# Mixture-of-experts stage of a decoder trunk: earlier conversion of the next down piece, combining between gate pieces, and a fifth pair of part buffers in place of a ring slot

## The chip, the cores and the metric

One core of one Trainium2 chip. The metric is the device time of one execution in microseconds; lower is better. The kernel before was timed in three runs.

## The reference, cut to what matters

Two layers of a decoder trunk on 256 tokens of width 1024, all in float32. Each layer has a mixer (attention beside a gated delta rule) and a channel mixer; the channel mixer of the second layer, which is what the change touches, sends each token to 2 of 8 experts:

```python
def swiglu(x, w_gate, w_up, w_down):
    return (jax.nn.silu(x @ w_gate) * (x @ w_up)) @ w_down

def moe_ffn(x, router_w, w_gate, w_up, w_down):
    logits = jnp.einsum('td,de->te', xf, router_w).astype(jnp.float32)
    top_val, top_idx = lax.top_k(logits, TOP_K)
    gates = jax.nn.softmax(top_val, axis=-1)
    ...
    y = y * w_buf[:, None].astype(y.dtype)
    out = jax.ops.segment_sum(y, tok_buf, num_segments=T)
```

An expert has two matrices of 1024 x 3584 (gate, up) and one of 3584 x 1024 (down).

## The kernel before

**Two parts of a weight.** TensorE multiplies in a rounded float32 form. To keep the full precision each weight is converted into two parts: ScalarE copies the raw weight to the rounded form, `wh` (L173), and VectorE subtracts it from the raw weight, which gives the rest, `wl` (L176). The activations are split the same way. A product with a weight is then TensorE's `wh` times both parts of the activation and `wl` times the first part. `halves` (L163) does this for one raw piece in two halves, each into a pair of buffers `wh`, `wl` from `wpool`, which has four pairs (`WB`).

**Loads.** `load` (L148) brings one raw piece into a slot: seven slots of `ring`, and in the expert stage also five of `ring2`, taken in the order of the string `SLOTS` (`r` and `x`). A slot is free again when VectorE has made the last `wl` of what lay in it. All loads are issued by SP in program order.

**The expert stage.** `experts` runs eight jobs, one an expert, in the order 0, 1, 4, 2, 5, 3, 6, 7 of the experts ranked by load. A wide job gives its tokens 128 rows; the three *narrow* ones (ranks 1 to 3) have at most 64 tokens and put the two parts of the activations side by side into one 128-wide operand, so that a weight half takes four matmuls of 448 columns instead of six. Each job has two chunks (`c`) of 1792 of the 3584 hidden columns. A chunk is: gate, eight rows `k` of 128 x 1792 (`in_pieces`), in banks `mm` and `gd` of PSUM; Silu copies of the four banks into `hh` (L1183); up, eight rows likewise; the product of both on VectorE (L1205); `to_features`, TensorE transposes of `hh` with their split into `hT` (L1131 to L1134).

**The pending down product.** The down product of a chunk is not made at once. It is kept in `pend` and its seven pieces of 2 x 1024 columns (`down_pieces`) are put between the gate and the up of the next chunk and behind them: `more()` takes the next piece, three of them around the Silu copies, the others after up.

**Copies of second parts.** In a narrow job the second parts' results lie in the upper 64 rows of the banks. The last row of gate and of up (`k = 7`) is not converted: TensorE multiplies the raw weights in full float32 into the lower 64 rows (`raw` in the trace). Just ahead of that, `leads` (L1108) lets ScalarE copy the upper rows out of the four banks (`room`, L1115, pinned in program order); four matmuls with a shifted identity (`move`) add them to the lower rows later. The bank's raw product waits for its room copy, because both touch that bank.

**Combining.** When the last down piece of an expert is done (in the first chunk of the next job), `combine` (L1086) splits the two result banks into `ys` (L1088, L1089), multiplies them with the transposed mask `DT` back to token order, and adds them, scaled, to `x_in` (L1095). Then `transposed` makes the next `DT`. The steps of `to_features` are kept as a list, `side`, and one is taken after each row of the next gate.

**Order.** The program is scheduled at build time: each engine gets one queue in a fixed order, which follows the order of the code as far as the scheduler's own estimate finds an instruction ready. Instructions wrapped in `pin` keep program order among themselves.

Of the kernel before, what the change touches and what calls it, by code (L numbers as in the profile page):

```python
# [10 lines left out]
F32R = mybir.dt.float32r  # L11
# [6 lines left out]
P = 128  # L18
# [17 lines left out]
C_COLS = C_SMALL * P + 32 + 6 * 32  # L36

RING = 7
RING2 = 5
SLOTS = "rrrrrxxxrrxx"  # L40
CHUNK = 1792
BANK = CHUNK // 4
NARROW = 3
# [24 lines left out]
def trunk(ctx, tc, x, positions, w_in, conv_w, a_log, dt_bias, gdn_norm_w, lam_q1, lam_k1, lam_q2, lam_k2,  # L68
# [7 lines left out]
    wpool = ctx.enter_context(tc.tile_pool(name="wpool", bufs=WB))  # L76
# [5 lines left out]
    def nm(s):  # L82
        cnt[0] += 1
        return f"{s}_{cnt[0]}"


    def bank(tag):
        return ps.tile([P, 512], F32, tag=tag, name=nm("ps_" + tag))
# [52 lines left out]

    WC, WH = 2048, 1040
    extra = []
    turn = [0]
    fence_high = [None]
    fence = [None]

# [15 lines left out]
    def halves(ld, cut=1, count=2):  # L163

        raw, nk, cols = ld
        m = nk * cols // count
        for i in range(count):
            wh = wpool.tile([P, WH], F32R, tag="wh", name=nm("wh"))
            wl = wpool.tile([P, WH], F32R, tag="wl", name=nm("wl"))
            n = m // (cut if i else 1)  # L170
            for c in range(0, m, n):
                w = raw[:, i * m + c:i * m + c + n]
                high = S.activation(wh[:, c:c + n], w, AF.Copy)  # L173
                if fence_high[0] is not None:
                    order(high, fence_high[0])
                low = V.tensor_tensor(wl[:, c:c + n], w, wh[:, c:c + n].bitcast(F32), op=ALU.subtract)  # L176
                if fence[0] is not None:
                    order(low, fence[0])
            yield i * (nk // count), wh, wl
# [796 lines left out]
    def experts(xs, jobs, mp, ring2, rest, first):  # L976
# [52 lines left out]
        def transposed(n):  # L1029
            Dt = mp.tile([P, NB, P], F32R, tag="ys", name=nm("D"))  # L1030
            slots(Dt, jobs[n], True)
            DT = mp.tile([P, NB, P], F32R, tag=f"DT{n % 2}", name=nm("DT"), bufs=1)
            pt = bank("a")
            for b in range(NB):
                PE.transpose(pt[:, b * P:(b + 1) * P], Dt[:, b].bitcast(F32), ident)
            V.tensor_copy(DT.rearrange("p b t -> p (b t)"), pt[:, 0:NB * P])
            return DT

# [24 lines left out]
        def down_pieces(n, c, first=0, parts=1, cut=1):  # L1063

            wd = weights(n, 2)[c * CHUNK:(c + 1) * CHUNK].rearrange("(p j) d -> p j d", j=NF)
            for f in range(first, NF, 2):
                yield [(f + j, wh, wl) for j, wh, wl in piece(wd[:, f:f + 2, :], 2, D, parts, cut if f == NF - 2 else 1)]

        def down(subs, n, c, hT, py):
            for f, wh, wl in subs:  # L1070
                K, k = NC * NF, c * NF + f
                if jobs[n][3]:
                    x_ = hT[:, f].rearrange("p c s -> p (c s)")
                    for w in (wh, wl):
                        for i, o in enumerate(py):
                            mm(o, x_, w[:, i * 512:(i + 1) * 512], k == 0 and w is wh, k == K - 1 and w is wl)
                else:
                    for w in (wh, wl):
                        for c_ in range(2 if w is wh else 1):
                            for i, o in enumerate(py):  # L1080
                                mm(o, hT[:, f, c_], w[:, i * 512:(i + 1) * 512], k == 0 and w is wh and c_ == 0,
                                   k == K - 1 and w is wl)

        def combine(n, py, DT):
            for i in range(2):
                ys = mp.tile([P, 2, 512], F32R, tag="ys", name=nm("ys"))  # L1086
                yh, yl = ys[:, 0], ys[:, 1]
                S.activation(yh, py[i], AF.Copy)  # L1088
                V.tensor_tensor(yl, py[i], yh.bitcast(F32), op=ALU.subtract)  # L1089
                for b in range(NB):  # L1090
                    pt = bank("a")
                    mm(pt, DT[:, b], yh, True, False)
                    mm(pt, DT[:, b], yl, False, True)
                    o = x_tok[:, b, i * 512:(i + 1) * 512]
                    V.scalar_tensor_tensor(o, pt, jobs[n][2][:, b], o, op0=ALU.mult, op1=ALU.add)  # L1095

        regs = {}

# [9 lines left out]
        def leads(banks):  # L1108

            hi = slice(64, P)  # L1110
            moves = []

            room = mp.tile([P, 4, BANK], F32R, tag=f"xg{(xg_turn[0] + 1) % 2}", name=nm("room"), bufs=1)
            for i, p in enumerate(banks):
                pin(S.activation(room[hi, i], p[hi, :], AF.Copy))  # L1115
                moves.append(lambda o=room[hi, i], p=p: mm(p[0:64, :], shift[hi, 0:64], o, False, True))
            return moves
# [24 lines left out]
        pend = None  # L1142
        side = []
# [5 lines left out]
        for n, job in enumerate(jobs):  # L1149
            narrow = job[3]  # L1150
            rows = slice(0, 64) if narrow else slice(0, P)
            xg = xgs.pop(n)
            x32 = as_one(xg) if narrow else None
            wg, wu = (weights(n, i).rearrange("(k p) c -> p k c", p=P) for i in range(2))
            for c in range(NC):
                banks = gu_banks()
                for k, f in enumerate(first or ()):
                    products(banks, xg, narrow, k, f)
                moves = ()
                for sub in in_pieces(wg, c, len(first or ()), narrow):  # L1160
                    if narrow and sub[0] == KD - 1:
                        moves = leads(banks)
                    products(banks, xg, narrow, *sub, x32)
                    if side:
                        side.pop(0)()
                first = None
                fence[0] = fence_high[0] = None
                while side:
                    side.pop(0)()
                hh = mp.tile([P, CHUNK], F32, tag="hh", name=nm("hh"))  # L1170
                downs = down_pieces(pend[0], pend[1]) if pend else iter(())

                def more():
                    subs = next(downs, None)
                    if subs:
                        down(subs, *pend)

                more()
                for move in moves:
                    move()  # L1180
                more()
                for i, p in enumerate(banks):
                    pin(S.activation(hh[rows, i * BANK:(i + 1) * BANK], p[rows, :], AF.Silu))  # L1183
                more()
                banks = gu_banks()
                if c == NC - 1 and groups and n + 1 not in xgs:
                    group = groups.pop(0)
                    tiles, side = dispatch([jobs[g] for g in group])
                    xgs.update(zip(group, tiles))
                moves = ()  # L1190
                for sub in in_pieces(wu, c, 0, narrow):
                    if narrow and sub[0] == KD - 1:
                        moves = leads(banks)
                    products(banks, xg, narrow, *sub, x32)
                    if side:
                        side.pop(0)()
                while side:
                    side.pop(0)()
                more()
                for move in moves:  # L1200
                    move()
                more()
                for i, p in enumerate(banks):
                    h = hh[rows, i * BANK:(i + 1) * BANK]
                    pin(V.tensor_tensor(h, h, p[rows, :], op=ALU.mult))  # L1205
                for subs in downs:
                    down(subs, *pend)
                if pend and pend[1] == NC - 1:
                    combine(pend[0], pend[3], DT)
                if c == 0:  # L1210
                    DT = transposed(n)
                    py = [bank("b"), bank("b")]
                hT, side = to_features(hh, narrow)
                pend = (n, c, hT, py)
        _, where, gate, _ = job
        while side:
# [5 lines left out]
        subs = [(f0 + f, wh, wl) for subs in down_pieces(n, c, NF - TAIL, 2, 2) for f, wh, wl in subs]  # L1222
# [187 lines left out]
                xT = finish(fp, *dense_ffn(0, xT, fp), ln2_g, ln2_b, l)  # L1410
    pre_ctx.close()
    with tc.tile_pool(name="ring2", bufs=RING2, reuse_waits="tile") as ring2, \
            tc.tile_pool(name="mp", bufs=1, side="right", reuse_waits="tile") as mp:
        extra.append(ring2)
        turn[0] = len(first)
        moe(xs, pl, first, mp, ring2)

# [26 lines left out]
```

## Time and profile before

| what | us |
|---|---|
| median of three runs | 1523.3 |
| the three runs | 1520.12, 1523.3, 1524.71 |
| profiled execution, its own time | 1522.21 |
| span of its profile, first to last instruction | 1520.1 |

The span is shorter than the time of the same execution by what lies around it. The expert stage takes about the last two thirds of the span. In the profile an engine is busy while it works on an instruction; a gap ahead of an instruction is named with what ended it. PE is TensorE's matmuls, PEld its weight loads, DVE VectorE, ACT ScalarE, SP the engine that issues the loads. Who ended a wait is inferred from semaphores and can be wrong where the engine or load that is named had long been done.

### The profile page before, as it was taken

What the parts mean: (1) busy time and instruction counts of PE and PEld (TensorE: products, weight loads), DVE (VectorE), ACT (ScalarE), POOL (GpSimd) and SP (SyncE); (2) the same over time, 40 slices, a digit from 0 to 9 for tenths busy, and PEclk for the clock granted to TensorE, in tenths of its full rate; (3) what the DMA queues carried; (4) which work ended last, traced back from release to release, by engine and by line L of the source; (5) the groups of instructions that cost most, each with busy time, mean ns of one, the idle gap of its engine ahead of it and who ended that gap; (6) DMA issues with size and microseconds to landing.
All of it is one profiled execution on the core that took longest, in us unless ns stands there. A gap on an engine that the chain in (4) does not pass through costs nothing.

```text
span 1520.1 us, 24270 instructions
## 1 busy us (share of the span) xinstructions
PE 1466.2 (96%) x8864; PEld 1227.9 (81%) x8864; DVE 1228.5 (81%) x1609; ACT 1068.5 (70%) x1553; POOL 23.8 (2%) x37
## 2 busy tenths in 40 slices
PE   8999999999999999999999999999999999999995
PEld 8968899998978889866688876588876678888884
DVE  5887655556796789988899888899888889898985
ACT  5747444456657388877787786887887778778773
POOL 1100000000100000000000000000000000000000
PEclk9999999999999899999999999999999999999998
DMA  9534455546532589998999999999999999999860
GB/s 327 204 113 124 157 192 194 185 123 215 170 103 105 194 325 366 337 399 316 396 415 339 365 360 344 395 391 351 380 350 370 352 381 405 340 348 369 310 281 32
DMA packets 89127, 433.95 MB, mean 285 GB/s; under 512 B 7816, under 2 KB 9992, under 8 KB 74912
## 3 DMA queue, kind: packets, MB, share of 16 engines
q1 hardware_dynamic: 87808, 428.54, 76.0%
q0 software_dynamic: 1184, 3.71, 0.8%
q8 instruction: 73, 1.20, 0.3%
q14 instruction: 62, 0.51, 0.1%
HBM read 431.17 MB, written 1.05 MB: 284 GB/s over the span
## 4 chain that ended last, share of the span: by engine, by line
PE 79%; DVE 9%; ACT 5%; DMA 4%; issue 2%; SPq 0%; DVEq 0%; ACTq 0%
PE ps_mm L101 23%; PE ps_gd L101 23%; PE ps_b L101 22%; PE ps_a L101 9%; DVE wl L176 6%; ACT wh L173 2%; DMA raw<-in_moe_w_up_dram 2%; DMA raw<-in_moe_w_down_dram 2%; PE ps_a L1131 2%; ACT hh L1183 1%; DVE hh L1205 0%; ACT room L1115 0%; DVE x_in L1095 0%; PE ps_mm L562 0%; DVE hT L1134 0%
## 5 line engine op out<-in xcount | busy, mean ns | idle before, releaser
L176 DVE TENSOR_TENSOR wl<-raw,wh 128x896 fp32r<-128x896 f32 (+2 forms) x851 | 938.8, 1144 | 199.3 <-ACT wh L173 182.6
L173 ACT ACTIVATE wh<-raw 128x896 fp32r<-128x896 f32 (+2 forms) x851 | 822.2, 997 | 236.3 <-PE ps_gd L101 91.1
L101 PE MATMUL ps_b<-wh,hT 128*128 128x512 f32 x816 | 233.7, 398 | 0.7 <-ACT hT L1133 0.7
L101 PE MATMUL ps_gd<-wh,xg 128*128 128x448 f32 x808 | 217.0, 368 | 0.0
L101 PE MATMUL ps_mm<-wh,xg 128*128 128x448 f32 x808 | 214.0, 372 | 1.0 <-ACT hh L1183 1.0
L101 PEld LDWEIGHTS ps_b<-wh,hT 128*128 128x128 f32 x816 | 151.8, 188 | 42.7 <-ACT wh L173 6.0
L101 PE MATMUL ps_b<-wl,hT 128*128 128x512 f32 x492 | 159.0, 403 | 5.8 <-DVE wl L176 5.8
L101 PEld LDWEIGHTS ps_gd<-wh,xg 128*128 128x128 f32 x808 | 152.5, 189 | 13.5
L101 PEld LDWEIGHTS ps_mm<-wh,xg 128*128 128x128 f32 x808 | 148.7, 190 | 15.3 <-ACT hh L1183 1.3
L101 PE MATMUL ps_gd<-wl,xg 128*128 128x448 f32 x488 | 146.6, 381 | 4.4 <-DVE wl L176 0.8
L101 PE MATMUL ps_mm<-wl,xg 128*128 128x448 f32 x488 | 144.7, 374 | 2.0 <-DVE wl L176 1.5
L101 PEld LDWEIGHTS ps_b<-wl,hT 128*128 128x128 f32 x492 | 89.9, 189 | 34.6 <-DVE wl L176 13.4
L101 PEld LDWEIGHTS ps_gd<-wl,xg 128*128 128x128 f32 x488 | 87.0, 189 | 37.1 <-DVE wl L176 22.6
L101 PEld LDWEIGHTS ps_mm<-wl,xg 128*128 128x128 f32 x488 | 89.4, 189 | 16.9 <-DVE wl L176 9.0
L101 PE MATMUL ps_mm<-xT,wh 128*128 128x256 f32 x448 | 70.9, 280 | 0.0
L101 PEld LDWEIGHTS ps_mm<-xT,wh 128*128 128x128 f32 x448 | 60.8, 189 | 0.4
L101 PE MATMUL ps_gd<-xT,wh 128*128 128x256 f32 x320 | 50.5, 280 | 0.0
L101 PE MATMUL ps_mm<-xT,wl 128*128 128x256 f32 x224 | 44.7, 280 | 0.0
L101 PEld LDWEIGHTS ps_gd<-xT,wh 128*128 128x128 f32 x320 | 43.1, 189 | 0.0
L1133 ACT ACTIVATE hT<-ps_a 128x512 fp32r<-128x512 f32 (+2 forms) x52 | 27.5, 540 | 21.6 <-PE ps_a L1131 14.1
L1131 PEld LDWEIGHTS ps_a<-cst,hh 128*128 128x128 f32 (+1 forms) x224 | 32.2, 200 | 6.3 <-DVE hh L1205 3.2
L1134 DVE TENSOR_TENSOR hT<-ps_a,hT 128x512 fp32r<-128x512 f32 (+2 forms) x52 | 31.8, 619 | 6.7 <-ACT hT L1133 6.6
(407 smaller groups left out, 1637.2 us busy)
## 6 DMA issues: line engine op xcount, KB each, us to landing
raw<-in_moe_w_gate_dram SPq DMA_DIRECT2D x128, 896.0 KB, 7.7
raw<-in_moe_w_up_dram SPq DMA_DIRECT2D x128, 896.0 KB, 6.7
raw<-in_moe_w_down_dram SPq DMA_DIRECT2D x110, 1024.0 KB, 7.7
raw<-in_w_in_dram SPq DMA_DIRECT2D x24, 1024.0 KB, 6.7
raw<-in_ffn_w_gate_dram SPq DMA_DIRECT2D x11, 1024.0 KB, 5.2
raw<-in_ffn_w_up_dram SPq DMA_DIRECT2D x11, 1024.0 KB, 5.1
raw<-in_ffn_w_down_dram SPq DMA_DIRECT2D x11, 1024.0 KB, 4.9
raw<-in_w_out_dram SPq DMA_DIRECT2D x8, 1024.0 KB, 4.9
```

The costliest lines, as they stand in the source:

```text
L101: return PE.matmul(o, lhsT, rhs, start=start, stop=stop, skip_group_check=True)
L173: high = S.activation(wh[:, c:c + n], w, AF.Copy)
L176: low = V.tensor_tensor(wl[:, c:c + n], w, wh[:, c:c + n].bitcast(F32), op=ALU.subtract)
L1131: PE.transpose(pt[:, f * w:(f + 1) * w], hv[:, f0 + f], ident[rows, rows])
L1133: S.activation(hT[:, f0:f0 + n_, 0], pv, AF.Copy)
L1134: V.tensor_tensor(hT[:, f0:f0 + n_, 1], pv, hT[:, f0:f0 + n_, 0].bitcast(F32), op=ALU.subtract)
L1183: pin(S.activation(hh[rows, i * BANK:(i + 1) * BANK], p[rows, :], AF.Silu))
```

## The change

Four edits, all in the expert stage. First, in a narrow job the next down piece is taken from `down_pieces` (its load issued and its two halves converted) ahead of `leads`, that is ahead of the room copies, for gate and for up; its products stay where they were. Second, `combine` returns its two halves as steps, which are appended to `side`, and so is the making of `DT`; they run one after each row of the next gate. `side` is begun after the second row of a gate instead of the first. The two accumulator banks of a down product are taken after that gate. Third, `halves` takes every fifth pair from a new pool of one pair, `wpool2`. Fourth, `ring2` has four slots instead of five, and `SLOTS` one letter less.

```diff
 RING = 7
-RING2 = 5
-SLOTS = "rrrrrxxxrrxx"
+RING2 = 4
+SLOTS = "rrrrrxxrrxx"
...
-    turn = [0]
+    turn = [0, 0]
...
         for i in range(count):
-            wh = wpool.tile([P, WH], F32R, tag="wh", name=nm("wh"))
-            wl = wpool.tile([P, WH], F32R, tag="wl", name=nm("wl"))
+            pool, size = wpool, WH
+            if extra:
+                turn[1] += 1
+                if turn[1] % 5 == 0:
+                    pool, size = extra[1], 1024
+            wh = pool.tile([P, size], F32R, tag="wh", name=nm("wh"))
+            wl = pool.tile([P, size], F32R, tag="wl", name=nm("wl"))
...
         def combine(n, py, DT):
-            for i in range(2):
+            def part(i):
                 ys = mp.tile([P, 2, 512], F32R, tag="ys", name=nm("ys"))
...
                     V.scalar_tensor_tensor(o, pt, jobs[n][2][:, b], o, op0=ALU.mult, op1=ALU.add)
+
+            return [lambda i=i: part(i) for i in range(2)]
...
-                moves = ()
+                downs = down_pieces(pend[0], pend[1]) if pend else iter(())
+                subs, moves = None, ()
                 for sub in in_pieces(wg, c, len(first or ()), narrow):
                     if narrow and sub[0] == KD - 1:
+                        subs = next(downs, None)
                         moves = leads(banks)
                     products(banks, xg, narrow, *sub, x32)
-                    if side:
+                    if side and sub[0]:
                         side.pop(0)()
...
-                downs = down_pieces(pend[0], pend[1]) if pend else iter(())
-
-                def more():
-                    subs = next(downs, None)
+                if pend and not pend[3]:
+                    pend[3].extend([bank("b"), bank("b")])
+
+                def more(subs=None):
+                    subs = subs or next(downs, None)
                     if subs:
                         down(subs, *pend)
 
-                more()
+                more(subs)
                 for move in moves:
                     move()
                 more()
...
-                moves = ()
+                subs, moves = None, ()
                 for sub in in_pieces(wu, c, 0, narrow):
                     if narrow and sub[0] == KD - 1:
+                        subs = next(downs, None)
                         moves = leads(banks)
...
-                more()
+                more(subs)
                 for move in moves:
                     move()
                 more()
...
+                hT, side = to_features(hh, narrow)
                 if pend and pend[1] == NC - 1:
-                    combine(pend[0], pend[3], DT)
+                    side += combine(pend[0], pend[3], DT)
                 if c == 0:
-                    DT = transposed(n)
-                    py = [bank("b"), bank("b")]
-                hT, side = to_features(hh, narrow)
+                    py = []
+                    later = []
+                    side.append(lambda n=n, later=later: later.append(transposed(n)))
+                else:
+                    DT = later[0]
                 pend = (n, c, hT, py)
...
     with tc.tile_pool(name="ring2", bufs=RING2, reuse_waits="tile") as ring2, \
+            tc.tile_pool(name="wpool2", bufs=1, reuse_waits="tile") as wpool2, \
             tc.tile_pool(name="mp", bufs=1, side="right", reuse_waits="tile") as mp:
-        extra.append(ring2)
+        extra.extend([ring2, wpool2])
```

## Rows read from the trace of the kernel before

**Rows 1.** The page: span, and busy time of each engine with its share.

```profile
span 1520.1 us, 24270 instructions
...
PE 1466.2 (96%) x8864; PEld 1227.9 (81%) x8864; DVE 1228.5 (81%) x1609; ACT 1068.5 (70%) x1553; POOL 23.8 (2%) x37
```

**Rows 2.** Busy time by stretch, one cycle: start:end, length, engines, granted clock, DMA.

```profile
core 0: us, PE busy (x) PEld busy (x) DVE busy (x) ACT busy (x) POOL busy (x), PEclk, DMA share, GB/s
862.40:893.40 31.00, 30.32 (x135) 22.71 (x134) 27.07 (x32) 23.65 (x31) 0.00 (x0) 1.00 0.93 343
893.40:921.00 27.60, 26.70 (x107) 18.25 (x106) 21.71 (x22) 22.99 (x30) 0.00 (x0) 1.00 0.99 382
921.00:955.10 34.10, 32.24 (x134) 21.84 (x132) 29.45 (x36) 23.59 (x30) 0.00 (x0) 1.00 0.91 326
955.10:982.80 27.70, 26.12 (x101) 16.82 (x101) 22.75 (x23) 23.67 (x30) 0.00 (x0) 1.00 1.01 397
982.80:1010.60 27.80, 27.15 (x135) 23.86 (x134) 27.43 (x30) 21.63 (x25) 0.00 (x0) 1.00 0.99 380
1010.60:1037.80 27.20, 26.68 (x127) 23.31 (x126) 24.96 (x24) 23.75 (x29) 0.00 (x0) 1.00 1.01 417
1037.80:1070.00 32.20, 30.85 (x149) 25.73 (x148) 31.68 (x39) 24.27 (x29) 0.00 (x0) 1.00 0.89 322
```

**Rows 3.** Waits in 862.4 to 1070 us: who, for whom: total, times, longest.

```profile
DVE wl L176 <- ACT wh L173: 20.4, 10, 3.9
...
PEld ps_gd L101 <- DVE wl L176: 8.0, 19, 0.6
...
PEld ps_b L101 <- DVE wl L176: 4.7, 8, 1.5
...
PEld ps_mm L101 <- DVE wl L176: 3.5, 8, 1.1
...
PEld ps_mm L101 <- ACT room L1115: 3.2, 4, 0.8
```

**Rows 4.** ScalarE's timeline from 941.75 us: start, length, instruction, [idle before].

```profile
941.75 3.88 ACT L173 ACTIVATE wh<-raw 128x896 fp32r<-128x896 f32 x4 [0.92 <-DVE wl L176]
948.15 0.97 ACT L1115 ACTIVATE room<-ps_mm 64x448 fp32r<-64x448 f32 x2 [2.52 <-PE ps_mm L101]
950.14 0.97 ACT L1115 ACTIVATE room<-ps_gd 64x448 fp32r<-64x448 f32 x2 [1.02 <-PE ps_gd L101]
951.14 3.90 ACT L173 ACTIVATE wh<-raw 128x1024 fp32r<-128x1024 f32 x4
```

**Rows 5.** VectorE's timeline at the same place.

```profile
940.49 8.10 DVE L176 TENSOR_TENSOR wl<-raw,wh 128x896 fp32r<-128x896 f32 x8
952.23 4.63 DVE L176 TENSOR_TENSOR wl<-raw,wh 128x1024 fp32r<-128x1024 f32 x4 [3.64 <-ACT wh L173]
957.95 3.36 DVE L176 TENSOR_TENSOR wl<-raw,wh 128x1024 fp32r<-128x1024 f32 x3 [1.09 <-ACT wh L173]
```

**Rows 6.** Waits of the whole span.

```profile
ACT room L1115 <- PE ps_mm L101: 30.4, 12, 2.8
...
ACT ys L1088 <- PE ps_b L101: 14.0, 7, 2.0
...
DVE hT L1134 <- ACT hT L1133: 6.6, 10, 1.6
```

**Rows 7.** SP's timeline of loads in the cycle: first issue, time to the last, count.

```profile
918.81 6.99 SPq L158 DMA_DIRECT2D raw<-in_moe_w_down_dram  x3
...
962.34 16.71 SPq L158 DMA_DIRECT2D raw<-in_moe_w_gate_dram  x8
```

**Rows 8.** Loads of the cycle (line 158): time from issue to landing.

```profile
DMA to landing us min/median/max: 4.6/7.3/9.9
```

**Rows 9.** VectorE's timeline at a combining.

```profile
929.95 0.69 DVE L1089 TENSOR_TENSOR ys<-ps_b,ys 128x512 fp32r<-128x512 f32 x1 [0.23 <-ACT ys L1088]
...
931.80 1.40 DVE L1095 SCALAR_TENSOR_TENSOR x_in<-ps_a,sorted,x_in 128x512 f32<-128x512 f32 x2
```

## The prediction

> **What bounds the kernel now.** I read the page first. TensorE is busy 96% of the span, VectorE 81%, ScalarE 70% [rows 1], which looks like a kernel at TensorE's limit. It is not quite: a matmul that waits for its weights counts its neighbours' overlap as busy, and the weight loader is only at 81% [rows 1]. So the second view is the table by stretches of one cycle of the expert stage (a narrow expert, 862.4 to about 982.8, and the wide one after it; there are three such cycles). Each stretch ends where the first Silu copy or the first gate-times-up product starts, so they alternate gate, up, gate, up. VectorE's idle time in them is length less busy: 3.9, 5.9, 4.7, 5.0 us in the four of the narrow expert, then 0.4, 2.2, 0.5 [rows 2]. The granted clock is 1.00, TensorE's 2.4 GHz level, so the clock explains nothing. Third, who waits: the weight loader waited 8.0 + 4.7 + 3.5 = 16.2 us of the 207.6 for `wl`, the low half that VectorE makes, and 3.2 for the room copies; VectorE itself waited 20.4 us in ten waits for ScalarE's `wh` [rows 3]. TensorE waits for VectorE, and VectorE for ScalarE.
>
> Fourth, the timeline at one of the places where that happens, 948 us. ScalarE finishes its last gate copy at 945.63, stands 2.52 us until TensorE has the first two banks ready, makes two room copies, stands 1.02, makes two more, and only then, at 951.14, starts the copies of the next down piece [rows 4]. VectorE ran out of `wh` at 948.59 and resumes at 952.23: 3.64 us idle [rows 5]. There are 12 such places (3 narrow experts, 2 chunks, gate and up); ScalarE's idle time before the first room copy is 30.4 us over the 12, 2.5 each [rows 6].
>
> **Copies of the next down piece ahead of the room copies.** Two `wh` copies take 1.95 us (half of 3.90 for four [rows 4]). They fit in the 2.52 that ScalarE stands there, with 0.57 to spare, so the room copies, and the raw products of TensorE that queue behind them, start when they do now. I cost the move at nothing on that path; without that cover it costs up to 1.95 us at each place (the slower rival, below). VectorE gets two `wl` of that piece, 2.31 us (half of 4.63 [rows 5]), straight after its last gate piece: its 3.64 us gap becomes about 1.3, ended by the second down piece. The loads don't move: the raw load of the last gate row is issued by then and the down piece's load is next on SP's queue, as before. The new wait on ScalarE's queue, for a free pair, stands ahead of the room copies; the pairs it needs were last read by the fifth and sixth rows of the gate, which TensorE has done.
>
> What of 2.31 reaches the end depends on what VectorE does until TensorE is next ahead of it. The four places of a cycle, in order:
> - gate of chunk 0: wide down pieces follow, on which TensorE is slower than VectorE, and the four Silu copies still block ScalarE. 0 to 2.3; I take 0.6.
> - up of chunk 0: the whole next stretch has 4.7 us of idle time, 3.64 of it at its own end, so VectorE sets the pace in it [rows 2, 5]. 1.0 to 2.3; I take 2.0.
> - gate of chunk 1: narrow down pieces and the up rows are VectorE-bound, but the Silu copies make VectorE wait once more (1.09 now [rows 5]), and that wait may grow. 1.0 to 2.3; I take 1.7.
> - up of chunk 1: the wide gate that follows has 0.4 us of idle time [rows 2], so all passes until TensorE is no longer behind. 0.5 to 2.3; I take 1.4.
>
> Sum 5.7 a cycle (2.5 to 9.2), three cycles: 17 us (7.5 to 27.6). It stays below the 16.2 us a cycle that the loader waits for `wl` [rows 3]. What is late next is the second down piece's copy behind the room copies, and the 3.2 us that the loader waits for the rooms themselves, which stay.
>
> **The fifth pair.** It lets ScalarE and VectorE be one half piece further ahead when a TensorE-bound stretch ends: 1.01 us (8.10 for eight [rows 5]). That counts where VectorE then runs without a break, as in the last stretch of the cycle (0.5 us idle [rows 2]), once, perhaps twice a cycle: 3 us, from 0 to 6.
>
> **The ring slot given up.** Eleven slots for twelve: each load is issued one piece later, some 2.1 us (16.71 for eight issues [rows 7]). The first down piece of the place above was issued at 918.81 [rows 7] and no load of the cycle took over 9.9 us to land [rows 8], so it lay ready by 928.7 and was copied from 951.14 [rows 4]: 22 us of reserve. Cost 0. The chain of waits books some microseconds to loads here; I don't believe it, since those landed long before. If the reserve were gone, each later load would cost its 2.1 us.
>
> **Results combined between pieces of the gate; transposes one row later.** Same instructions, other places. ScalarE no longer stands for the last down product before `ys` (14.0 us in 7 waits [rows 6]); but VectorE felt only 0.23 of one such wait [rows 9], so the gain is at most 7 x 0.23 = 1.6. What it may cost: steps of this form, product, ScalarE copy, VectorE rest, stand between pieces already (four in each of 10 wide chunks, two in each of 6 narrow ones: 52) and cost VectorE 6.6 us [rows 6], 0.13 each; 7 x 3 new ones, 2.7. Value 0, from -1.6 to +2.7. The scaled sums into `x_in`, 1.40 a pair [rows 9], stay on VectorE and are only spread. The mask's transposes move with them, and the two accumulator banks are taken after the gate, ahead of the first product that writes them. Behind these steps in VectorE's queue stand `wl` copies that run ahead of TensorE, which is why I price a wait there at VectorE's own tenth and not at TensorE's.
>
> **Sum.** 17 + 3 + 0 = 20 us off. The profiled execution took 1522.2 us (span 1520.1 [rows 1]); 1502.2 follows. The median of the runs is 1.1 above it, less than their own spread, so I say 1502. With all bounds at their ends: 1522.2 - 27.6 - 6 - 1.6 = 1487, and 1522.2 - 7.5 - 0 + 2.7 = 1517.4; the likeliest case's own range is 1490 to 1514.
>
> **Rivals.**
> *The gain stays in front of TensorE.* VectorE is early at the 12 places, but the Silu copies and the wide down pieces take it back, and only the second place of each cycle pays: 3 x 2.0 = 6, so 1516 (1513 to 1518). For it: at two of four places what follows is TensorE-bound or blocked. Against it: 16.2 us of waits for `wl` a cycle.
> *Loads become the bound.* The stage moved 343, 382, 326, 397, 380, 417 and 322 GB/s in the seven stretches [rows 2]. If about 360 is all that the memory gives over a stage, any microsecond gained waits for loads again, and with a smaller ring the end is where it is: 1522, no change. The trace is against it: 417 over 27 us, and 22 us of reserve at each load; I give it 4 in 100. The Trainium skill speaks for it: "Perfetto Trace Analysis", section Roofline, gives a core 358 GB/s of memory as its share and a ceiling near 435 when it is alone; by the first figure there is nothing to win. The 417 GB/s row is above that share, so here the second applies.
> *The edit is eaten elsewhere.* The order of instructions on each queue shifts all through the stage, and new waits of a few tenths at 12 places and 7 combinings (about 1 us each) cancel the 20: 1519 to 1527.
> *Room copies come late (slower).* Place: ScalarE's queue at the 12 places. If the two copies can't start in the 2.52 us, because the pair that they want is still read by TensorE, they run when the room copies run now. TensorE's raw products wait 1.95 longer, 12 x 1.95 = 23.4, and VectorE gains only 2.31 - 1.95 = 0.36 a place, 4: 1522.2 + 23.4 - 4 - 3 = 1539. It is a matter of how late: each place loses what the slip exceeds the 0.57, so with 20 us of gain to eat the sign turns at a slip of 20 / 12 = 1.7 us. For it: `wh` copies wait for TensorE elsewhere. Against: at 945.6 four older halves have been through TensorE.
>
> **How the numbers follow.** Forecast 0.61, mostly below 1514 and with some 0.05 below 1490; gain stays in front 0.14; loads 0.04; eaten 0.09; slower 0.12. About 0.3% (4.6 us) can be told from no change here. Faster by more than that: 0.61 + 0.14 and a little of the eaten case, 0.76; same: 0.12; slower 0.12. The range takes in the bounds below and the cases up to no change: 1487 to 1522, leaving out the slower case, its neighbours and a thin tail below.
>
> **What would show it.** In the profile after: ScalarE's wait before `room` (30.4 us) down to some 7 (12 x 0.57) while the room copies start no later after the last gate `wl`; VectorE's gap at those places about 1.3 instead of 3.6; the loader's wait for `wl` down by a third or more; narrow stretches 1.5 to 2.5 us shorter each, and the last wide gate of the cycle about 1. Wrong if the wait before `room` has stayed, if the loader's wait for the room copies has grown well above 3.2 us a cycle, or if loads appear as releasers of ScalarE's copies with landing just before.

## The result

The changed kernel took 1498.5 us (median of four runs, 1496.95 to 1498.59). The kernel before, timed beside it, took 1522.9 (1520.12 to 1524.71). The ratio is 0.9839 with a 95% interval of 0.9822 to 0.9856, 24.4 us less. A microsecond or two of that may be the clock's (an estimate): among 23 other runs of the kernel before, the four shortest (1517.8 to 1519.1 us) had a mean granted clock of 0.986 to 0.989 and the four longest (1524.1 to 1525.4) of 0.980 to 0.985, against 0.985 to 0.988 in the runs of the changed kernel. The forecast was 1502, with 1490 to 1514 as its likeliest range, so sign and size were right. The terms behind the size were not all right, and that is what the rest of this document is about.

### The profile page after: what moved, and what is told of

It reads as the page before. It is cut to its first block, busy times and chain, and to the rows that moved or that the text cites. A ratio compares the mean times of both kernels' runs of the same rounds, so it can differ in the third digit from the quotient of the medians.

```text
span 1496.4 us, 24248 instructions
## 1 busy us (share of the span) xinstructions
PE 1451.6 (97%) x8864; PEld 1233.7 (82%) x8864; DVE 1225.9 (82%) x1609; ACT 1054.2 (70%) x1553; POOL 23.8 (2%) x37
## 4 chain that ended last, share of the span: by engine, by line
PE 86%; DVE 6%; ACT 3%; issue 2%; DMA 2%; SPq 0%; DVEq 0%; ACTq 0%
PE ps_b L101 25%; PE ps_mm L101 25%; PE ps_gd L101 24%; PE ps_a L101 9%; DVE wl L181 4%; PE ps_a L1138 2%; DMA raw<-in_moe_w_up_dram 1%; ACT wh L178 1%; DVE x_in L1100 0%; PE ps_mm L567 0%; DMA x_in<-in_x_dram 0%; ACT junk L416 0%; ACT hh L1193 0%; PE ps_gd L409 0%; PE ps_mm L671 0%
## 5 line engine op out<-in xcount | busy, mean ns | idle before, releaser
L178 ACT ACTIVATE wh<-raw 128x896 fp32r<-128x896 f32 (+2 forms) x851 | 808.2, 996 | 201.2 <-PE ps_gd L101 79.0
L101 PEld LDWEIGHTS ps_gd<-wh,xg 128*128 128x128 f32 x808 | 151.6, 188 | 13.1
L101 PE MATMUL ps_gd<-wl,xg 128*128 128x448 f32 x488 | 142.9, 373 | 9.3 <-DVE wl L181 7.5
L101 PE MATMUL ps_mm<-wl,xg 128*128 128x448 f32 x488 | 140.8, 369 | 0.1
L101 PEld LDWEIGHTS ps_b<-wl,hT 128*128 128x128 f32 x492 | 90.8, 188 | 32.2 <-DVE wl L181 6.7
L1141 DVE TENSOR_TENSOR hT<-ps_a,hT 128x512 fp32r<-128x512 f32 (+2 forms) x52 | 31.9, 621 | 16.6 <-ACT hT L1140 16.5
```

The source lines that it names most:

```text
L101: return PE.matmul(o, lhsT, rhs, start=start, stop=stop, skip_group_check=True)
L1141: V.tensor_tensor(hT[:, f0:f0 + n_, 1], pv, hT[:, f0:f0 + n_, 0].bitcast(F32), op=ALU.subtract)
```

## The profile after

The page answers to [rows 1]. This profiled execution took 1498.59 us.

```profile
span 1496.4 us, 24248 instructions
...
PE 1451.6 (97%) x8864; PEld 1233.7 (82%) x8864; DVE 1225.9 (82%) x1609; ACT 1054.2 (70%) x1553; POOL 23.8 (2%) x37
```

The same matmuls and the same VectorE instructions; the span lost 23.7 us. The busy time of those 8864 matmuls fell by 14.6 us (1466.2 to 1451.6), so more than half of what was lost had been booked as busy. The table by stretches of the same cycle answers to [rows 2], with the same columns and the same events as bounds.

```profile
855.50:886.50 31.00, 30.75 (x141) 24.02 (x140) 29.77 (x34) 25.64 (x35) 0.00 (x0) 1.00 0.92 339
886.50:911.10 24.60, 24.60 (x107) 18.64 (x105) 21.45 (x22) 22.65 (x29) 0.00 (x0) 1.00 1.01 418
911.10:944.80 33.70, 31.72 (x136) 22.84 (x135) 30.55 (x36) 22.37 (x29) 0.00 (x0) 1.00 0.97 369
944.80:969.40 24.60, 23.70 (x93) 15.58 (x92) 21.03 (x20) 22.95 (x30) 0.00 (x0) 1.00 1.00 391
969.40:997.40 28.00, 28.00 (x135) 23.97 (x134) 25.43 (x28) 20.04 (x25) 0.00 (x0) 1.00 0.99 386
997.40:1023.90 26.50, 26.50 (x128) 23.63 (x127) 25.54 (x25) 23.40 (x29) 0.00 (x0) 1.00 1.01 420
1023.90:1054.20 30.30, 30.30 (x150) 26.72 (x149) 29.13 (x36) 23.20 (x31) 0.00 (x0) 1.00 0.98 378
```

Read the lengths against [rows 2]: 31.0, 24.6, 33.7, 24.6, 28.0, 26.5, 30.3 for 31.0, 27.6, 34.1, 27.7, 27.8, 27.2, 32.2. The cycle takes 198.7 us for 207.6. Both up stretches of the narrow expert are 3 us shorter; its gates are nearly as they were. The second of the two also holds 8 matmuls fewer (93 for 101), which now stand in other stretches, so its length alone overstates what was gained there. The last wide gate lost 1.9. The waits of the cycle answer to [rows 3], who, for whom, total, times, longest:

```profile
DVE wl L181 <- ACT wh L178: 10.1, 13, 3.2
PEld ps_gd L101 <- DVE wl L181: 6.9, 11, 1.6
...
PEld ps_mm L101 <- DVE wl L181: 1.5, 5, 0.4
PEld ps_mm L101 <- ACT room L1122: 1.4, 5, 0.4
PEld ps_b L101 <- DVE wl L181: 0.9, 2, 0.4
```

VectorE's wait for `wh` has halved (20.4 before). The loader waits 9.3 us for `wl` (16.2 before) and 1.4 for the rooms (3.2 before). At the place that the prediction took apart, ScalarE's timeline answers to [rows 4]:

```profile
930.10 5.36 ACT L178 ACTIVATE wh<-raw 128x896 fp32r<-128x896 f32 x6
937.43 0.97 ACT L1122 ACTIVATE room<-ps_mm 64x448 fp32r<-64x448 f32 x2 [1.97 <-PE ps_mm L101]
938.76 0.97 ACT L1122 ACTIVATE room<-ps_gd 64x448 fp32r<-64x448 f32 x2 [0.36 <-PE ps_gd L101]
939.76 2.95 ACT L178 ACTIVATE wh<-raw 128x1024 fp32r<-128x1024 f32 x3
944.79 0.97 ACT L1193 ACTIVATE hh<-ps_mm 64x448 f32<-64x448 f32 x2 [2.08 <-PE ps_mm L101]
```

and VectorE's to [rows 5]:

```profile
937.12 3.36 DVE L181 TENSOR_TENSOR wl<-raw,wh 128x896 fp32r<-128x896 f32 x3
940.85 3.50 DVE L181 TENSOR_TENSOR wl<-raw,wh 128x1024 fp32r<-128x1024 f32 x3 [0.38 <-ACT wh L178]
947.60 6.24 DVE L181 TENSOR_TENSOR wl<-raw,wh 128x1024 fp32r<-128x1024 f32 x6 [3.25 <-ACT wh L178]
```

VectorE's gap ahead of the down pieces fell from 3.64 to 0.38 us. The next one, behind the Silu copies, grew from 1.09 to 3.25: of 4.73 us idle, 3.63 are still there, a little later. The waits of the whole span that answer to [rows 6], and one that was 0.8 in 3 waits before:

```profile
ACT ys L1093 <- PE ps_b L101: 16.3, 7, 4.4
...
DVE hT L1141 <- ACT hT L1140: 16.5, 20, 3.1
...
ACT room L1122 <- PE ps_mm L101: 12.7, 10, 2.0
...
PE ps_gd L101 <- DVE wl L181: 7.5, 12, 1.2
```

ScalarE's wait ahead of the rooms is 12.7 for 30.4. The two that the second edit bears on did not fall: 16.3 for 14.0 ahead of `ys`, and VectorE's wait for `hT`, of the transposes, 16.5 for 6.6. The loads of the cycle, from issue to landing, answer to [rows 8]:

```profile
DMA to landing us min/median/max: 4.7/8.2/11.6
```

They take 0.9 us longer in the median, and in the cycle VectorE waited for a load only twice, 0.6 us together. The stretches carry up to 420 GB/s. So the ceiling near 435 in the Trainium skill, "Perfetto Trace Analysis", section Roofline, fits this trace too, and the share of 358 GB/s bound nothing here: six of the seven stretches stand above it.

## The experiments

Times are medians of all runs of a kernel, five rounds each, and the differences are to the kernel before timed beside it (1521.9 to 1522.5 us). "The stage" is, here and below, the time in the profile from the first Silu copy of the first expert to the last gate-times-up product of the last one: 917.9 us in the kernel before, 890.9 in the changed one.

### Each edit alone

The first edit alone:

```diff
+                        subs = next(downs, None)
                         moves = leads(banks)
...
-                more()
+                more(subs)
```

> The kernel before with one part of the change: the next down piece taken ahead of the room copies, in gate and in up. Theory (the copies fill ScalarE's 2.5 us wait at the 12 places): 17 us less than before, some 1506, from 7.5 to 27.6; the wait before room falls from 30.4 to about 7 us. Rival (the fifth pair is what counts, the copies wait for a free pair without it): at most 5 us less, above 1517. Rival (the spread combining is what counts): no more than 5 us less.

It took 1509.3 us, ratio 0.9913 [0.9897, 0.9929], 13.1 off. ScalarE's wait before the first room copy went from 30.4 to 5.9 us; the prediction said some 7.

The second edit alone:

```diff
-                    combine(pend[0], pend[3], DT)
+                    side += combine(pend[0], pend[3], DT)
...
-                    DT = transposed(n)
+                    side.append(lambda n=n, later=later: later.append(transposed(n)))
```

> The kernel before with the combining and the mask's transposes as steps between gate rows, the steps begun one row later, the accumulator banks taken after the gate. Theory: no change, 1521 to 1526. Rival (spread combining counts, because ScalarE no longer stands 2 us for ys at each of 7 combinings): 6 us less or more, below 1517.

1522.4 us, 1.0004 [0.9991, 1.0017]: nothing.

The third and fourth together (`turn[1] % 5 == 0` takes the pair from `wpool2`, `RING2 = 4`):

> The kernel before with the fifth pair of part buffers and eleven ring slots instead of twelve. Theory: 3 us less, 0 to 6, so 1517 to 1523. Rival (the fifth pair is what counts): 10 us less or more, below 1513. Rival (loads become the bound with eleven slots): 2 us a piece where it binds, above 1526.

1512.2 us (1506.75 to 1515.24), 0.9928 [0.9908, 0.9948], 10.3 off. The forecast for this edit was 3, from 0 to 6. The fourth alone:

```diff
-RING2 = 5
-SLOTS = "rrrrrxxxrrxx"
+RING2 = 4
+SLOTS = "rrrrrxxrrxx"
```

> The kernel before with eleven ring slots instead of twelve and nothing in their place. Theory (22 us of reserve at the loads): no change, within 2 us of before. Rival (loads are near the bound): 4 us more or above, since one load cycle of 2.1 us is lost in each of the stretches that draw the ring down.

1520.8 us, 0.999 [0.9978, 1.0003]: nothing, so the 10.3 are the pair's own.

Where they lie, the table by stretches shows. First the wide expert 4 of the kernel before, gate, up, gate:

```profile
743.20:770.90 27.70, 27.07 (x135) 23.86 (x134) 27.39 (x30) 21.61 (x25) 0.00 (x0) 1.00 0.99 387
770.90:798.00 27.10, 26.58 (x127) 23.32 (x126) 24.92 (x24) 23.74 (x29) 0.00 (x0) 1.00 1.01 417
798.00:830.20 32.20, 30.85 (x149) 25.74 (x148) 31.72 (x39) 24.33 (x30) 0.00 (x0) 1.00 0.90 324
```

then the same with the fifth pair alone:

```profile
744.90:771.50 26.60, 25.94 (x129) 22.88 (x129) 26.60 (x30) 21.25 (x26) 0.00 (x0) 1.00 1.00 389
771.50:797.80 26.30, 26.30 (x128) 23.65 (x127) 25.09 (x25) 23.39 (x29) 0.00 (x0) 1.00 1.01 417
797.80:828.70 30.90, 30.63 (x148) 25.67 (x147) 30.41 (x38) 23.97 (x30) 0.00 (x0) 1.00 0.92 345
```

1.1, 0.8 and 1.3 us: about the 1.01 us of one half piece, in each of three wide stretches and not in one. That makes 3.2 a cycle and some 10 in three. All nine such stretches of the three cycles sum to 262.7 us before and 253.2 with the pair, 9.5 less; in each profile one of the nine, a first gate, had a mean granted clock of 0.94 and is longer than its two likes (29.2 for 27.7 and 27.8; 28.1 for 26.6 and 26.5).

### The places of the copies ahead

The prediction gave a cycle 0.6 + 1.7 for the two gate places and 2.0 + 1.4 for the two up places. So the first edit was made at the six gate places alone, and at the six up places alone.

> The kernel before with the next down piece ahead of the room copies in the gate only (6 of 12 places). As the prediction had it (0.6 + 1.7 us a cycle): 7 us less, 1515. Rival (what follows a gate is the Silu copies, which wait for the moves, so what is gained there is kept: the up stretches shortened by 2.6 and 3.1 with all 12): 11 us less, 1511, and nearly all of the 13.

1513.5 us, 0.9945 [0.9929, 0.996], 9.1 off.

> The kernel before with the next down piece ahead of the room copies in the up only (the other 6 places). As the prediction had it (2.0 + 1.4 us a cycle): 10 us less, 1512. Rival (the gate places hold nearly all): 2 us less, 1520.

1515.5 us, 0.9948 [0.993, 0.9966], 7.0 off. Both kinds pay alike within these intervals, and the two sum to 16.1, 3 more than the whole edit, about what the intervals leave open. A split of 7 to 10 is neither shown nor excluded; that one kind holds nearly all of it is excluded.

### Do late room copies cost?

The slower rival said that TensorE stands while the room copies are late. So two down pieces, not one, were converted ahead of them, with four pairs:

```diff
-                        subs = next(downs, None)
+                        subs = [x for _ in range(2) for x in next(downs, None) or ()]
```

> As e1 (the kernel before, four pairs, twelve slots), but with two down pieces instead of one ahead of the room copies. The third and fourth copies need the pairs of the last gate row, which TensorE lets go of only when the first room copies could run, so the room copies come late: the slower rival of the prediction, brought about on purpose. By its price (TensorE's raw products wait as long as the rooms slip, 2 us or more at each of 12 places): 24 us above e1, 1530 to 1537, slower than before, the loader's wait for room up from 4 us to 25 or more. Rival (TensorE has other products to do there, as the down product that it now makes while it waits for the rooms): within 6 us of e1, below 1516.

1512.7 us (1507.93 to 1514.18), 0.993 [0.9915, 0.9945]: 9.2 off, not slower. ScalarE's timeline at the place first, with seven conversions (three of the gate, four of the down pieces) ahead of the rooms and no idle time in front of them:

```profile
940.21 7.05 ACT L173 ACTIVATE wh<-raw 128x896 fp32r<-128x896 f32 x7 [0.86 <-DVE wl L176]
947.29 0.97 ACT L1115 ACTIVATE room<-ps_mm 64x448 fp32r<-64x448 f32 x2
948.16 0.97 ACT L1115 ACTIVATE room<-ps_gd 64x448 fp32r<-64x448 f32 x2
```

and TensorE's:

```profile
946.17 0.67 PE L101 MATMUL ps_gd<-wl,xg 128*128 128x448 f32 x2
947.30 0.73 PE L101 MATMUL ps_b<-wl,hT 128*128 128x512 f32 x2 [0.46 <-DVE wl L176]
947.87 0.62 PE L101 MATMUL ps_b<-wh,hT 128*128 128x512 f32 x2
...
950.00 1.34 PE L101 MATMUL ps_mm<-raw,xg 128*64 128x448 f32 x3
```

The raw products start at 950.00, 2.7 us after the first room copy began, and TensorE has done down products (`ps_b`) until then. It stood for 0.46 us. With four pairs, though, a second piece ahead brings nothing more: its waits for `wl` grew (table below).

### The set without the spread combining

> The changed kernel without the spread combining (copies ahead, fifth pair, eleven slots). Theory (the parts add, the spread is worth nothing): 24 us less than before, 1496 to 1501. Rival (the spread is worth something once the others are in, since the fifth pair lets ScalarE run further ahead and into the wait for ys): 3 us or more slower than the changed kernel, above 1502. Second rival (the spread costs by then, the waits for hT and ys in the changed kernel's trace having grown): below 1495.

1494.6 us (1494.07 to 1495.87), 0.982 [0.9805, 0.9835]: 27.9 off, 4 us under the changed kernel. The runs of the two don't overlap (each was timed beside the kernel before, but not beside the other); the intervals of their ratios do. In the profiles the stage takes 888.1 us for 890.9. The stretches show one price in the narrow expert's second gate, which is where the combining now stands. Without the spread it takes

```profile
909.70:942.50 32.80, 31.71 (x136) 22.79 (x136) 30.43 (x36) 22.71 (x29) 0.00 (x0) 1.00 0.95 366
```

for 33.7 in the changed kernel, while the wide second gate takes 31.0 for 30.3 there. So the spread loses 0.9 in a narrow gate and wins 0.7 in a wide one, and over three cycles these two nearly cancel. The rest of the 2.8 us lies elsewhere: 0.3 in the up stretch after each of the three wide gates, 1.1 in the last expert and 0.3 in the first. A kernel that spreads only in wide jobs except the last follows from that:

```diff
-        if pend and pend[1] == NC - 1:
-            combine(pend[0], pend[3], DT)
+        late = combine(pend[0], pend[3], DT) if pend and pend[1] == NC - 1 else []
+        spread = None if narrow or n == NE - 1 or c else late
+        if spread is None:
+            for step in late:
+                step()
...
```

> As e5 (copies ahead, fifth pair, eleven slots), with the spread combining only in the gates of wide jobs but the last, and combining at once in the narrow ones. The stretches of the traces of the changed kernel and of e5 say that the spread makes a narrow gate of the second chunk 0.85 us longer (33.7 for 32.85) and a wide one 0.65 shorter (30.3 for 30.95). Theory (it is this simple): 3 x 0.65 = 2 us less than e5, 1492 to 1494, and 5 us below the changed kernel. Rival (noise of a single trace): as e5, 1494 to 1496.

1492.8 us (1490.51 to 1495.42), 0.9811 [0.9797, 0.9825]. That is the expected direction against the 1494.6, but less than the runs differ among themselves. The stage takes 887.2 us for 888.1: the wide gates win 0.7 each, as expected, and the up stretches behind them lose 0.3 each, which the expectation left out. So the gain is about 1 us by the profiles, and not settled by the times.

### More pairs

The kernel before with six pairs and ten slots (`wpool2` with two pairs, `RING2 = 3`):

```diff
-                if turn[1] % 5 == 0:
+                if turn[1] % 6 >= 4:
                     pool, size = extra[1], 1024
```

> The kernel before with six pairs and ten ring slots instead of four and twelve. Theory (each pair lets VectorE be one half piece, 1 us, ahead at each place where a TensorE-bound stretch ends, three in a cycle and some after): about twice the 10 us of one pair, less what is no longer to be had: 14 to 18 us less, 1504 to 1508. Rival (the first pair alone unlocks it): as with five pairs, 1511 to 1513. Rival (loads bind with ten slots): above 1514.

1505.2 us, 0.9891 [0.9876, 0.9906], 17.3 off: the sixth pair gives some 7 more, and a second ring slot less, which was not run by itself, costs nothing that shows. Then six pairs with the copies ahead and without the spread:

> As e5, with six pairs and ten ring slots. Theory (the sixth pair gives on top of the copies ahead what it gave without them, 1512.2 to 1505.2): 7 us less than e5, 1487 to 1490. Rival (the copies ahead use up the idle time of VectorE that the sixth pair would have filled): 2 us less or none, 1493 to 1495. Rival (loads bind at ten slots when the rest is faster): above 1496.

1488.2 us (1486.18 to 1491.95), 0.9781 [0.9767, 0.9795]: the fastest kernel of the study, 10 us below the changed one and 34 below the one before. With the spread in wide jobs added:

> All that helped together: copies ahead, six pairs, ten slots, spread combining in wide jobs but the last. Theory (the parts add): 2 us less than e11. Rival (with six pairs VectorE is far enough ahead that the spread no longer matters): as e11 within 1 us.

1489.4 us (1485.93 to 1494.27), 0.979 [0.9772, 0.9808], the same as without it.

### What TensorE waited for, over all kernels

Who waited for what is the view that ties these together. TensorE and its weight loader together, in the whole span, summed from the rows of the waits in which PE or PEld waits for `wl` or for `room`; the time is the profiled execution's own, which differs from the median. One standstill can be in both counts: at 948.74 us in the kernel before, the loader waits 0.80 us and the matmuls 0.42 for the same room copy. So these sums put kernels in order; they are not microseconds of the time.

```text
kernel                              wl     room   sum    us (profiled)
before                              53.7   17.8   71.5   1522.2
spread alone                        58.8   19.0   77.8   1523.3
eleven slots alone                  54.7   17.8   72.5   1523.6
ahead in gate                       55.5   11.1   66.6   1511.8
ahead in up                         55.0   12.0   67.0   1515.3
copies ahead                        57.2    4.3   61.5   1509.3
two pieces ahead                    60.4    1.1   61.5   1513.5
fifth pair                          36.9   19.9   56.8   1515.2
six pairs                           34.0   17.1   51.1   1505.1
the change                          42.3    4.1   46.4   1498.6
the change without the spread       38.9    4.3   43.2   1494.4
... spread in wide jobs only        37.3    4.3   41.6   1492.4
six pairs, copies ahead             32.4    4.8   37.2   1486.2
... spread in wide jobs only        34.3    4.8   39.1   1489.4
```

The columns fall apart by edit. Copies ahead take the waits for rooms away, by half when made at half the places, and raise those for `wl` a little. Pairs take the waits for `wl` away and leave the rooms. The sum falls by 25.1 us in the changed kernel, which is 23.6 faster by the profiled executions; from before to the last-but-one row by 34.3 for 36.0. With waits counted twice, that these figures lie so close is in part chance. Elsewhere they don't: copies ahead alone lose 10.0 of waits and 12.9 of time, the fifth pair 14.7 of waits and 7.0 of time (10.3 by the medians, 9.8 in the stage), and the spread alone adds 6.3 of waits and nothing to the time. The rows of the rooms in the kernel before are

```profile
PEld ps_mm L101 <- ACT room L1115: 9.1, 12, 0.8
...
PE ps_mm L101 <- ACT room L1115: 4.7, 11, 0.4
...
PEld ps_gd L101 <- ACT room L1115: 4.0, 14, 0.3
```

and with the copies ahead alone one is left:

```profile
PEld ps_mm L101 <- ACT room L1115: 4.3, 15, 0.4
```

## Why the prediction came out as it did

**Copies ahead: 17 predicted, 13 measured, in good part by another road.** That the two conversions fit into ScalarE's 2.52 us was right (30.4 to 5.9 us). But the argument went on from VectorE: 2.31 us earlier, hence a third less waiting for `wl`. That step failed. With this edit alone the waits for `wl` did not fall at all, 53.7 to 57.2. (In the cycle of the changed kernel they did fall by more than a third, 16.2 to 9.3, but that came with the fifth pair.) What fell were the waits for the rooms, 17.8 to 4.3, of which the prediction said that they stay. It looked only at the raw product that waits for a room copy, and not at what else TensorE could then do. TensorE's timeline at the place, before:

```profile
947.64 0.68 PE L101 MATMUL ps_mm<-wl,xg 128*128 128x448 f32 x2
948.74 0.96 PE L101 MATMUL ps_mm<-raw,xg 128*64 128x448 f32 x2 [0.42 <-ACT room L1115]
949.64 0.68 PE L101 MATMUL ps_gd<-wl,xg 128*128 128x448 f32 x2
950.24 0.97 PE L101 MATMUL ps_mm<-raw,xg 128*64 128x448 f32 x2
951.04 1.67 PE L101 MATMUL ps_gd<-raw,xg 128*64 128x448 f32 x4
...
974.72 0.97 PE L101 MATMUL ps_mm<-raw,xg 128*64 128x448 f32 x2 [0.43 <-ACT room L1115]
```

and with the copies ahead alone:

```profile
944.05 0.68 PE L101 MATMUL ps_gd<-wl,xg 128*128 128x448 f32 x2 [0.33 <-DVE wl L176]
944.56 0.63 PE L101 MATMUL ps_b<-wh,hT 128*128 128x512 f32 x2
945.18 0.51 PE L101 MATMUL ps_b<-wl,hT 128*128 128x512 f32 x1
945.62 1.72 PE L101 MATMUL ps_mm<-raw,xg 128*64 128x448 f32 x4
947.17 1.67 PE L101 MATMUL ps_gd<-raw,xg 128*64 128x448 f32 x4
...
970.26 1.72 PE L101 MATMUL ps_mm<-raw,xg 128*64 128x448 f32 x4
```

Before, the raw product comes straight behind its bank's last gate product and waits. With the edit, three down products stand between, since their halves are converted by then, and the raw products run in one piece. The prediction said that the products stay where they were; in the code they do, in TensorE's queue they moved.

How much this filling gave can be estimated from these lines. At a place it saves the wait of 0.42, and the eight raw products take 3.15 us in one piece, up to the start of what follows, for 3.90 with two gate products (0.60) between them: some 0.6 a place, 7 us over the 12, about half of the 13. From the first raw product of this place to that of the next, with 92 matmuls in both kernels, TensorE took 24.6 us for 26.0: 1.3 less, and 0.6 of it is one place. The other half arose between the places, where the waits for `wl` moved without becoming less in sum. No run held TensorE's order fixed, so how much of it VectorE's earlier start gave is not shown.

**The four places.** 0.6, 2.0, 1.7 and 1.4 were put on the stretch behind each place. With the edit alone the stretches behind them changed by -2.6, -0.4, -3.1 and +1.4 (25.0, 33.7, 24.6 and 29.2 for 27.6, 34.1, 27.7 and 27.8). The sum, 4.7 for 5.7, was sized well; the split was not, and "narrow stretches 1.5 to 2.5 shorter each" was wrong. These lengths themselves mislead, because matmuls moved across their bounds: 107, 134, 101 and 135 before, 105, 138, 93 and 141 with the edit. From the first raw product of one place to that of the next, at an estimated 0.25 us for each matmul more or less (two start 0.50 apart in the lines above), the edit at the gate places alone gave 1.3 behind each of the two, and at the up places alone 1.3 behind the first and 0.6 behind the second, for 0.6, 1.7, 2.0 and 1.4.

**The fifth pair: 3 predicted, 10 measured.** This is the term that was mis-sized. The size of one place, a half piece, was right. The count was wrong: one stretch a cycle, where VectorE was seen to run without a break, and three it was. The middle wide stretch, with 2.2 us of VectorE's idle time, paid 0.8 as well.

**The ring slot: 0 predicted, 0 measured.** The rival of the loads falls with it. The 2.1 us for an issue was low, 16.71 over seven intervals is some 2.3, but nothing hung on it.

**The spread combining: 0 predicted.** Alone it is 0, but not because nothing happened. With the spread alone the second gates of the same cycle, narrow and wide, are

```profile
923.10:958.00 34.90, 32.24 (x135) 21.62 (x133) 29.45 (x36) 22.89 (x29) 0.00 (x0) 1.00 0.92 320
1040.80:1071.80 31.00, 30.88 (x149) 26.25 (x147) 30.08 (x37) 23.61 (x29) 0.00 (x0) 1.00 0.96 354
```

for 34.1 and 32.2 before [rows 2]: 0.8 lost in the narrow one, 1.2 won in the wide one. The prediction priced a new wait at VectorE's tenth, because `wl` copies run ahead of TensorE. That step failed in the narrow gates, in the old kernel already: TensorE's waits for `wl` ahead of `ps_gd` go from 0.8 us in 3 waits to 5.7 in 12 with the spread alone, and from 2.9 in 9 to 7.5 in 12 with the spread added to the other edits. In the changed kernel the loss is still 0.9, but the win is 0.7; the fifth pair by itself has brought the wide gate to 31.0, and less is left to win. The smaller win is the larger part of why the spread costs 2.8 us of the stage there (about 4 by the medians, past the bound of 2.7); the rest is spread over stretches of a few tenths. VectorE's longer wait for `hT` is mostly not the spread's: it is 13.2 us without it and 4.1 with the spread alone.

**That the sum was right is partly luck.** Alone, the edits gave 13.1 + 10.3 + 0 = 23.4. Together the first and third gave 27.9, and the second took 4 back. The pair alone changed nothing between the raw products of the second and the third narrow expert; with the copies ahead it took another 1.0 and 0.6 us a cycle there (24.8 to 23.8 and 34.7 to 34.1), which is about what the two give beyond their sum. Against forecasts of 17, 3 and 0, one error of -4 and one of +7 stand side by side.

**The slower rival** had its price from TensorE standing while the rooms are late. Two pieces ahead made them late, and TensorE did not stand.

## What to carry to other kernels

Where an engine with a fixed queue waits for a short copy, look for work that could be made ready for that moment: filling the wait gave about half of the gain here, and the prediction had put it at nothing. When a buffer is added between two engines, count every stretch in which the one ahead could be a piece further, also those in which it shows some idle time: each paid about one piece here, and six pairs paid more than five. An edit that measures as nothing alone can be a loss and a win that cancel: look at it by stretches, and take it out of the finished set once more. The spread combining came out even in the old kernel and not in the new one. And before the length of a stretch is read as a gain, count the instructions in it.

## What was not expected of the hardware

What surprised was a row: TensorE's matmuls were busy 96% of the span before [rows 1], and 36 us of the profiled execution could still be taken out (1522.2 to 1486.2). 21 of them came out of the busy time of the same 8864 matmuls (1466.2 to 1444.8), so part of what counts as busy is waiting. The Trainium skill, "Perfetto Trace Analysis", section Identifying the Most-Contended Engine, says that the busy time of matmuls is no good measure for this and names that of weight loads, beside the share of the peak arithmetic, as a better one. On the matmuls the traces agree: they stand at 97% in the fastest kernel. Weight loads went from 81% to 83%; how good a measure they are, no run here shows.

The clock, which the prediction put at nothing from one cycle at 1.00, has a price elsewhere in the stage that rows show: a wide first gate of the kernel before took 29.2 us at a mean of 0.94, for 27.7 and 27.8 at 1.00. From 1227.3 to 1230.7 us TensorE had its 1.2 GHz level there; just before, it had stood for 0.63 us and made 14 small transposes.
